# Hybrid encoder trunk on one core: other places for the norm vectors, a later place for the first ReLU tiles, another order of the first weights of the mixers

## The chip, the cores and the metric

The kernel runs on one NeuronCore of a Trainium2 chip. The metric is the device time of one execution in microseconds (us), as the median of several executions. The core has a matrix engine (PE in the profile, TensorE), a vector engine (DVE), a scalar engine (ACT), a general engine (POOL) and an engine that only issues transfers here (SP). They run side by side, each through its own list of instructions in order, and meet only at semaphores: an instruction that waits holds all that stand behind it on its engine.

## What is computed

Two layers of an encoder over 256 tokens of width 1024, in float32. Each layer norms the tokens, feeds three mixers (an mLSTM, a Fourier mixer and a state-space mixer, S5), projects their gated sum, adds it through a second norm, and does the same with a squared-ReLU MLP:

```python
for l in range(DEPTH):                      # DEPTH = 2
    h = rmsnorm(x, g_mix_pre[l])
    z = h @ w_in[l] + b_in[l]               # 1024 -> 5904 columns: q, k, v, o, gates, ...
    ...                                     # y_m, y_f, y_s: mLSTM, Fourier, S5
    mixed = gates[..., 0, :] * y_m + gates[..., 1, :] * y_f + gates[..., 2, :] * y_s
    x = x + rmsnorm(mixed @ w_out[l], g_mix_post[l])
    h = rmsnorm(x, g_ffn_pre[l])
    f = square(relu(h @ w_ffn1[l])) @ w_ffn2[l]     # 1024 -> 4096 -> 1024
    x = x + rmsnorm(f, g_ffn_post[l])
```

## The kernel before

**Products in three parts.** Every float32 factor is split into a high part (`hi`) and a low part (`lo`), and a product is done as hi x hi, hi x lo and lo x hi (`mm3`, lines 273 to 275 of the profile, or the same three in `tokens`, line 289, and `last`, line 311). A weight tile is loaded as `raw` by SP (line 211), copied to `whi` by ACT (line 213), and `wlo` = `raw` - `whi` is done by DVE (line 215). `raw`, `whi` and `wlo` are rings of a few slots: a load waits until DVE has done with the slot it takes, a split until PE has.

**Tokens** are two tiles of 128 rows, t0 and t1. `x_sb` holds x. Where a stage ends, `norms` (lines 397 to 442) does for each tile: a sum of squares of the two halves of the result (ACT, line 405 or 407), the reciprocal root on POOL, the product with the vector of the norm behind the stage (DVE, line 409), the sum into x (line 416), and the product with the vector of the norm ahead of the next stage (line 421, or 377 in a mixer). The normed tile is then turned by eight PE transposes (line 192), whose result is split into `hT_5` (hi) and `hT_6` (lo) by ACT (line 391 or 394) and DVE (line 392 or 395).

**The order there** is written out by hand. `meet` runs over a string, `MEET[0]` at the end of a mixer, `MEET[1]` at the end of an MLP: `0` and `1` are the next step of `norms` for t0 and t1, `P` the products that are left for t1, `h` and `l` the hi and the lo of the next weight tile of the stage that comes (`after`, a `Feed`). In it ACT and DVE follow the written order; elsewhere a scheduler orders the instructions of all engines by its own estimate.

**The start of the MLP.** The first 768 of the 4096 hidden columns are done with the tokens as the standing factor (`tokens`), as a group of 512 (weight tiles in the places `QT0`, `QT1`, `Wt0`, `Wt1`) and a group of 256 (`tabC`/`tabS` and a ring tile), whose splits can be done ahead. For t0 and then t1 the products go to two banks (`mm`), the ReLU to `w2k` (ACT, line 1272), its square (DVE, line 1273), six PE transposes (line 192, out `mm`) turn it, and the result is split into `ringB` (ACT line 1260, DVE line 1261). The rest of the columns (`f1`, chunks of 256) have the weights standing, 48 products of 256 columns each; `f2(kk)` does the second product for 128 hidden columns and both token tiles, 12 products of 512 columns. The scheduler puts `f2` of the first tiles between them.

**The vectors of the norms** are loaded for all partitions (512 KB each) into one pair, a tile of the ring A, by SP at the end of the stage (lines 467 and 470). Ring A has three slots; the S5 loads (lines 637 and 642) take one as well. `Tt`, `oth` and `gx` are places that the mixers use and the MLP does not.

**The first weights of a mixer** (`mixer_units`) are three tiles of the gates and the Fourier columns (`igf`, 272 columns) and four of v (512 columns; 128 x 1024 each), in that order; in layer 1 the first v tile lies in a `whi`/`wlo` slot, the other three in the rings A, A and B.

Of the kernel before, what the change touches and what calls it, by code (L numbers as in the profile page):

```python
# [15 lines left out]
P = 128  # L16
# [40 lines left out]

MEET = ("000Ph11l101", "hl0h0llP0101h11")

# [59 lines left out]
def encoder_kernel(ctx: ExitStack, tc: tile.TileContext, a: dict, out: bass.AP):  # L119
# [152 lines left out]
    def mm3(o, lhi, llo, rhi, rlo, start, stop):  # L272
        mm(o, lhi, rhi, start=start, stop=False)  # L273
        mm(o, lhi, rlo, start=False, stop=False)  # L274
        mm(o, llo, rhi, start=False, stop=stop)  # L275

    def tokens(t, parts, together, step=NK // 2):

        tt = slice(t * P, (t + 1) * P)
        todo = []
        for then, n, units, kn in parts:
            ps = mm_ps()
            o = ps[:, :n]

            def part(a, i, ks, last=False):
                for k in ks:
                    mm(o, a[:, k, tt], units[k // kn][i][:, k % kn, :], start=k == 0 and a is hhi and i == 0,  # L289
                       stop=last and k == NK - 1)  # L290

            for k0 in range(0, NK, step):
                ks = range(k0, min(k0 + step, NK))
                part(hhi, 0, ks)
                if t > 0:
                    part(hhi, 1, ks)
                part(hlo, 0, ks, t > 0)
            if t > 0:
                then(t, ps)
            else:  # L300
                todo.append((then, ps, o, units, kn))
            if not together:
                last(t, todo)
        last(t, todo)
# [77 lines left out]
    def spread(hs, t, scale):  # L382

        for c in range(2):
# [5 lines left out]
            if scale is None:  # L390
                act(o[0], p3, AF.Copy)
                V.tensor_sub(o[1], p3, o[0].bitcast(F32))
            else:
                act(o[0], p3, AF.Copy, scale=scale)
                stt(o[1], p3, scale, o[0].bitcast(F32), ALU.mult, ALU.subtract)

    def norms(t, ps, gpost, gpre, owed=None, lend=None):
# [5 lines left out]
        for c in range(2):  # L403
            if owed is None:
                act(junk(), ps[c], AF.Square, accum_out=ss[:, c:c + 1])
            else:
                act(junk(), ps[c], AF.Square, scale=owed[t][0], accum_out=ss[:, c:c + 1])  # L407
            f = w2k()
            stt(f, ps[c], ROOT_D if owed is None else owed[t][1], gpost[:, half(c)], ALU.mult, ALU.mult)
            fg.append(f)  # L410
        rs = rstd_of(ss)
        yield
# [10 lines left out]
        if lend is not None:  # L423
            yield
            spread(hs, t, None)
            yield
# [35 lines left out]

    def load_gains(gpre, gpost, between=lambda: None):

        gg = ring("A", [P, 2, D])
        if gpost is not None:
            nc.sync.dma_start(gg[:, 1, :], gpost.partition_broadcast(P))
        between()
        if gpre is not None:
            nc.sync.dma_start(gg[:, 0, :], gpre.partition_broadcast(P))  # L470
        return gg
# [562 lines left out]
    def mixer_units(l, iu, vu):  # L1034

        w = a["w_in"][l]
        rings = [None] * 4 if l == 0 else [None, "A", "A", "B"]
        return Feed([(iu, pieces_of(w, k0, min(3, NK - k0), OFF_IG, NIGF)) for k0 in (0, 3, 6)] +
                    [(vu, (*pieces_of(w, k0, 2, OFF_V, M_ML), rings[k0 // 2])) for k0 in range(0, NK, 2)])

    def mixer(l, iu, vu, after, owed):
# [166 lines left out]

        wunits(range(NK))
        gg = load_gains(a["g_ffn_pre"][l], a["g_mix_post"][l], after.load)  # L1210
        for _ in range(5):
            after.lo()
        aps = [[acc_ps(t) for _ in range(2)] for t in range(NT)]

# [38 lines left out]
    def ffn(l, groups, after, owed):  # L1253
# [148 lines left out]
```

## Time and profile before

| what | value |
|---|---|
| median of 3 executions | 836.88 us (836.64 to 836.92) |
| profiled execution | 836.79 us, of which the span of the trace is 835.0 us |
| PE busy in the span | 806.5 us (97%) |
| DVE, ACT, POOL busy | 597.8 (72%), 472.2 (57%), 33.2 us (4%) |
| mean granted clock of PE | 0.995 of full speed |

The table says that PE is the engine whose idle time and clock matter; the others wait most of the time for it or for transfers.

### The profile page before, as it was taken

What the parts mean: (1) busy time and instruction counts of PE and PEld (TensorE: products, weight loads), DVE (VectorE), ACT (ScalarE), POOL (GpSimd) and SP (SyncE); (2) the same over time, 40 slices, a digit from 0 to 9 for tenths busy, and PEclk for the clock granted to TensorE, in tenths of its full rate; (3) what the DMA queues carried; (4) which work ended last, traced back from release to release, by engine and by line L of the source; (5) the groups of instructions that cost most, each with busy time, mean ns of one, the idle gap of its engine ahead of it and who ended that gap; (6) DMA issues with size and microseconds to landing.
All of it is one profiled execution on the core that took longest, in us unless ns stands there. A gap on an engine that the chain in (4) does not pass through costs nothing.

```text
span 835.0 us, 14911 instructions
## 1 busy us (share of the span) xinstructions
PE 806.5 (97%) x5825; PEld 746.1 (89%) x5825; DVE 597.8 (72%) x1071; ACT 472.2 (57%) x784; POOL 33.2 (4%) x63
## 2 busy tenths in 40 slices
PE   7999999998979999999989999999999899999996
PEld 5899999998868999999868999999997699999995
DVE  4999899887783576677568798776987555555563
ACT  4668764676553447567654355666855344444451
POOL 1000200010020000000010010000000100000000
PEclk9999999999999999999999999999999999999999
DMA  8775844554862665756736554555667356666541
GB/s 263 223 225 143 246 121 119 158 163 151 279 176 75 187 191 147 245 166 199 260 111 205 175 178 128 151 177 154 180 200 250 102 171 184 195 184 199 180 176 50
DMA packets 122262, 147.87 MB, mean 177 GB/s; under 512 B 22310, under 2 KB 104398, under 8 KB 121936
## 3 DMA queue, kind: packets, MB, share of 16 engines
q1 hardware_dynamic: 122044, 146.66, 57.5%
q8 instruction: 45, 0.74, 0.4%
q10 hardware_dynamic: 148, 0.27, 0.1%
q14 instruction: 25, 0.20, 0.1%
HBM read 144.33 MB, written 2.57 MB: 176 GB/s over the span
## 4 chain that ended last, share of the span: by engine, by line
issue 43%; PE 24%; DVE 3%; DMA 3%; ACT 2%; POOL 1%; DVEq 0%; POOLq 0%
PE mm L273 5%; PE mm L274 5%; PE mm L275 5%; PE mm L289 3%; DMA raw<-in_w_ffn_dram 2%; DMA raw<-in_w_out_dram 1%; DVE wlo L215 1%; PE acc L793 1%; PE mm L311 1%; PE acc L990 1%; DVE x_sb L416 1%; PE acc L192 1%; POOL rs L358 0%; POOL rs L356 0%; PE acc L829 0%
## 5 line engine op out<-in xcount | busy, mean ns | idle before, releaser
L215 DVE TENSOR_TENSOR wlo<-raw,whi 128x1024 fp32r<-128x1024 f32 (+1 forms) x231 | 280.2, 1217 | 146.9 <-ACT whi L213 145.4
L213 ACT ACTIVATE whi<-raw 128x1024 fp32r<-128x1024 f32 (+1 forms) x231 | 242.1, 1053 | 232.0 <-PE mm L274 139.2
L273 PE MATMUL mm<-hT,whi 128*128 128x256 f32 x1024 | 289.2, 282 | 0.0
L275 PE MATMUL mm<-hT,wlo 128*128 128x256 f32 x1024 | 288.9, 282 | 0.0
L274 PE MATMUL mm<-hT,whi 128*128 128x256 f32 x1024 | 288.7, 282 | 0.0
L273 PEld LDWEIGHTS mm<-hT,whi 128*128 128x128 f32 x1024 | 193.1, 189 | 1.5
L274 PEld LDWEIGHTS mm<-hT,whi 128*128 128x128 f32 x1024 | 192.8, 188 | 1.1
L275 PEld LDWEIGHTS mm<-hT,wlo 128*128 128x128 f32 x1024 | 193.1, 189 | 0.2
L274 PE MATMUL acc<-wlo,ringB 128*128 128x512 f32 x280 | 109.0, 390 | 0.0
L275 PE MATMUL acc<-whi,ringB 128*128 128x512 f32 x280 | 108.3, 390 | 0.0
L273 PE MATMUL acc<-whi,ringB 128*128 128x512 f32 x280 | 107.1, 391 | 0.7 <-ACT ringB L1260 0.7
L275 PEld LDWEIGHTS acc<-whi,ringB 128*128 128x128 f32 x280 | 52.5, 188 | 11.2
L273 PEld LDWEIGHTS acc<-whi,ringB 128*128 128x128 f32 x280 | 52.6, 188 | 11.0 <-ACT ringB L1260 1.0
L274 PEld LDWEIGHTS acc<-wlo,ringB 128*128 128x128 f32 x280 | 52.6, 188 | 9.9
L957 DVE SCALAR_TENSOR_TENSOR t1k<-ringB,pc,t1k 128x254 f32<-128x254 f32 (+1 forms) x64 | 31.0, 484 | 0.9
L289 PE MATMUL mm<-whi,hT 128*128 128x272 f32 (+2 forms) x136 | 29.3, 338 | 1.4 <-ACT whi L213 0.8
L273 PE MATMUL mm<-ringB,whi 128*128 128x256 f32 x96 | 27.4, 286 | 1.7 <-ACT ringB L1027 1.7
L274 PE MATMUL mm<-ringB,whi 128*128 128x256 f32 x96 | 27.3, 284 | 0.0
L275 PE MATMUL mm<-ringB,wlo 128*128 128x256 f32 x96 | 27.2, 284 | 0.0
L356 POOL TENSOR_SCALAR rs<-ss 128x1 f32<-128x1 f32 x16 | 6.6, 415 | 488.6 <-ACT t1k L407 345.7
L289 PEld LDWEIGHTS mm<-whi,hT 128*128 128x128 f32 x136 | 22.2, 202 | 4.2 <-ACT whi L213 1.1
L273 PEld LDWEIGHTS mm<-ringB,whi 128*128 128x128 f32 x96 | 18.3, 191 | 2.0 <-ACT ringB L1027 1.9
(355 smaller groups left out, 1144.0 us busy)
## 6 DMA issues: line engine op xcount, KB each, us to landing
raw<-in_w_ffn_dram SPq DMA_DIRECT2D x128, 512.0 KB
raw<-in_w_in_dram SPq DMA_DIRECT2D x84, 512.0 KB
raw<-in_w_out_dram SPq DMA_DIRECT2D x16, 512.0 KB
raw<-in_w_glu_dram SPq DMA_DIRECT2D x16, 256.0 KB
raw<-in_w_up_mlstm_dram SPq DMA_DIRECT2D x8, 512.0 KB
ringB<-md SPq DMA_DIRECT2D x2, 1024.0 KB
raw<-in_w_up_fourier_dram SPq DMA_DIRECT2D x4, 512.0 KB
raw<-in_w_in_dram SPq DMA_DIRECT2D x4, 408.0 KB
```

The lines of the kernel that those rows point to most:

```text
L192: nc.tensor.transpose(o, i, cst[:k, C_ID:C_ID + k])
L213: act(hi, raw, AF.Copy)
L215: latest[0] = V.tensor_sub(lo, raw, hi.bitcast(F32)).ins
L273: mm(o, lhi, rhi, start=start, stop=False)
L274: mm(o, lhi, rlo, start=False, stop=False)
L275: mm(o, llo, rhi, start=False, stop=stop)
L289: mm(o, a[:, k, tt], units[k // kn][i][:, k % kn, :], start=k == 0 and a is hhi and i == 0, stop=last and k == NK - 1)
L311: mm(o, hhi[:, k, tt], units[k // kn][1][:, k % kn, :], start=False, stop=k == NK - 1)
L416: stt(xv, fg[c], rs, xv, ALU.mult, ALU.add)
L793: mm(bps[:, (g * 2 + r) * JN:(g * 2 + r + 1) * JN], QT[r][:, g0 + g, :], U[:, 4 * b + g, :], start=True, stop=True, skip_group_check=True)
L957: stt(u[:, lo_:hi_], z[:, lo_ + o:hi_ + o], col(l, "cw", j * 8 + i), u[:, lo_:hi_], ALU.mult, ALU.add)
L990: mm(nps[:, d * 256:d * 256 + DH + 1], pt[d, j][:, t * P:(t + 1) * P], v_sb[:, j, h, :], start=i == 0, stop=i == len(js) - 1, skip_group_c ...
```

## The change

No instruction is added or removed; places and orders change.

1. `load_gains` puts each vector into a place of its own: the one behind the mixers into `Tt`, the one ahead of the MLP into `oth`, the one behind the MLP into `oth`, the one ahead of the next mixer into `gx`. SP no longer issues them at the end of the stage, between weight tiles, but as soon as the place is free.
2. `MEET[0]` and `norms`: both sums of squares come first (the product of line 409 stands a step later), and further splits of the MLP's weights stand behind the norms.
3. In the MLP the ReLU tiles of t0 (`done`) and all that follows from them are issued behind all products of t1; those of t1 behind the first `f1` chunk; the sum of squares of x (line 429, `rest`) behind the t0 tiles. `tc.issue_after(i)` only says that what follows stands behind `i` in the schedule.
4. `mixer_units` of layer 1: the first v tile (in ring A) comes second, the next in the `whi`/`wlo` slot; `MEET[1]` splits it ahead of the norms, and the other three between t0's transposes and t1's second norm.

```diff
-MEET = ("000Ph11l101", "hl0h0llP0101h11")
+MEET = ("000P101lh1l1", "hlhl00h0lhlP1001hhh1ll1l1")
...
     def norms(t, ps, gpost, gpre, owed=None, lend=None):
...
+        rs = rstd_of(ss)
+        yield
+        for c in range(2):
             f = w2k()
             stt(f, ps[c], ROOT_D if owed is None else owed[t][1], gpost[:, half(c)], ALU.mult, ALU.mult)
             fg.append(f)
-        rs = rstd_of(ss)
         yield
...
-            spread(hs, t, None)
+            ends[:2] = spread(hs, t, None)
...
-    def load_gains(gpre, gpost, between=lambda: None):
-
-        gg = ring("A", [P, 2, D])
-        if gpost is not None:
-            nc.sync.dma_start(gg[:, 1, :], gpost.partition_broadcast(P))
-        between()
-        if gpre is not None:
-            nc.sync.dma_start(gg[:, 0, :], gpre.partition_broadcast(P))
+    def load_gains(gpost, gpre, tags):
+
+        gg = []
+        for g, tag in zip((gpost, gpre), tags):
+            gg.append(None)
+            if g is not None:
+                gg[-1] = per([P, D], tag)
+                nc.sync.dma_start(gg[-1], g.partition_broadcast(P))
         return gg
...
-        rings = [None] * 4 if l == 0 else [None, "A", "A", "B"]
+        rings = [None] * 4 if l == 0 else ["A", None, "A", "B"]
...
+        if l > 0:
+            specs.insert(1, specs.pop(3))
...
+        gpost, gpre = load_gains(a["g_mix_post"][l], a["g_ffn_pre"][l], ("Tt", "oth"))
         mix = [ring("B", [P, NK, S], F32R) for _ in range(2)]
...
-        for _ in range(5):
+        for _ in range(4):
             after.lo()
+        after.hi()
...
-        parts = [(hidden(f0, n), n, units, kn) for f0, n, kn, units in groups]
+        done = []
+
+        def later(then):
+            return lambda t, ps: done.append((then, t, ps))
+
+        parts = [(later(hidden(f0, n)), n, units, kn) for f0, n, kn, units in groups]
         for t in range(NT):
             tokens(t, parts, True)
+
+        behind = ExitStack()
+        for i in ends:
+            behind.enter_context(tc.issue_after(i))
+        for _ in groups:
+            then, t, ps = done.pop(0)
+            then(t, ps)
+        for chain in owed.pop("rest"):
+            next(chain, None)
...
             f1(c)
+            if c == first:
+                with tc.issue_after(ends[2]):
+                    for then, t, ps in done:
+                        then(t, ps)
+                behind.close()
...
+        gpost, gpre = load_gains(a["g_ffn_post"][l], None if last else a["g_mix_pre"][l + 1], ("oth", "gx"))
```

The changed code has lines of its own: L406, L392, L432 of the change are L405, L391, L429 of before (the sum of squares, hT's hi, the sum of squares of x), L1279 and L1267 are L1272 and L1260 (ReLU, ReLU tile's hi), L290 and L312 are L289 and L311, L274 to L276 are L273 to L275.

**ACT where layer 0 goes from the mixers to the MLP.** Before; `acc_2926` and `acc_2927` are the projection of t0, `acc_2928` and `acc_2929` that of t1, `w2k_3171` is the first ReLU tile:

```order
L405 ACTIVATE t1k_2991,ss_2986<-acc_2927 128x512
L391 ACTIVATE hT_5_84<-acc_3005 128x4x128
L391 ACTIVATE hT_5_84<-acc_3012 128x4x128
L213 ACTIVATE whi_2921<-raw_2920 128x1024
L405 ACTIVATE t1k_3063,ss_3062<-acc_2928 128x512
L405 ACTIVATE t1k_3067,ss_3062<-acc_2929 128x512
L213 ACTIVATE whi_3271<-raw_3270 128x1024
L213 ACTIVATE whi_3301<-raw_3300 128x1024
L213 ACTIVATE whi_3338<-raw_3337 128x1024
L1272 ACTIVATE w2k_3171<-mm_3129 128x512
L391 ACTIVATE hT_5_84<-acc_3082 128x4x128
L391 ACTIVATE hT_5_84<-acc_3089 128x4x128
```

After:

```order
L406 ACTIVATE t1k_2989,ss_2986<-acc_2927 128x512
L406 ACTIVATE t1k_3048,ss_3047<-acc_2928 128x512
L406 ACTIVATE t1k_3050,ss_3047<-acc_2929 128x512
L392 ACTIVATE hT_5_84<-acc_3056 128x4x128
L392 ACTIVATE hT_5_84<-acc_3063 128x4x128
L213 ACTIVATE whi_2922<-raw_2921 128x1024
L392 ACTIVATE hT_5_84<-acc_3083 128x4x128
L392 ACTIVATE hT_5_84<-acc_3090 128x4x128
L1279 ACTIVATE w2k_3200<-mm_3100 128x512
```

Both sums of t1 now stand ahead of t0's hT; three splits that stood ahead of the first ReLU tile are gone from there. They stand here now (`whi_3254`, `whi_3284` of `f1`, `whi_3339`, `whi_3357` of `f2`):

```order
L1279 ACTIVATE w2k_3210<-mm_3117 128x256
L432 ACTIVATE t1k_3236,ss_3233<-x_sb_78 128x512
L213 ACTIVATE whi_3254<-raw_3253 128x1024
L213 ACTIVATE whi_3284<-raw_3283 128x1024
L213 ACTIVATE whi_3339<-raw_3338 128x1024
L213 ACTIVATE whi_3357<-raw_3356 128x1024
L1267 ACTIVATE ringB_3098<-mm_3203 128x4x128
L1267 ACTIVATE ringB_3099<-mm_3213 128x2x128
```

That is ahead of the hi of t0's ReLU tiles (`ringB_3098`, `ringB_3099`), where before nothing stood between the last ReLU and that hi.

**PE at the start of the MLP of layer 0.** Before: from t1's transposes (`acc_3082`, `acc_3089`) to its first products:

```order
L192 MATMUL acc_3082<-cst_79,w2k_3076 128x128 x4
L192 MATMUL acc_3089<-cst_79,w2k_3079 128x128 x4
L311 MATMUL mm_3146<-wlo_2922,hT_5_84 128x256 x4
L192 MATMUL mm_3174<-cst_79,w2k_3171 128x128 x4
L273 MATMUL acc_3265<-whi_3338,ringB_3127 128x512
L274 MATMUL acc_3265<-wlo_3339,ringB_3127 128x512
L273 MATMUL acc_3266<-whi_3338,ringB_3127 128x512
L274 MATMUL acc_3266<-wlo_3339,ringB_3127 128x512
L192 MATMUL mm_3192<-cst_79,w2k_3189 128x128 x2
L289 MATMUL mm_3197<-QT_459_2896,hT_5_84 128x512 x2
```

After: the end of t1's products, t0's ReLU transposes, the first products of `f2`, and the first of `f1` (`mm_3252`):

```order
L290 MATMUL mm_3175<-whi_2922,hT_5_84 128x256 x4
L290 MATMUL mm_3175<-wlo_2923,hT_5_84 128x256 x4
L290 MATMUL mm_3175<-whi_2922,hT_6_85 128x256 x4
L192 MATMUL mm_3203<-cst_79,w2k_3200 128x128 x4
L192 MATMUL mm_3213<-cst_79,w2k_3210 128x128 x2
L274 MATMUL acc_3248<-whi_3339,ringB_3098 128x512
L275 MATMUL acc_3248<-wlo_3340,ringB_3098 128x512
L274 MATMUL acc_3249<-whi_3339,ringB_3098 128x512
L275 MATMUL acc_3249<-wlo_3340,ringB_3098 128x512
L274 MATMUL mm_3252<-hT_5_84,whi_3254 128x256
```

What stood between t1's transposes and its products (ReLU transposes, four products of `f2`) now stands behind the products, and the transposes of t1's ReLU tile are not here but behind the first `f1` chunk and `f2` of t0.

**PE at the start of the mixers of layer 1.** Before; `mm_5148` is the bank of t0's `igf` products, `mm_5174` that of its v products, `acc_5112` and `acc_5119` are t1's transposes:

```order
L289 MATMUL mm_5148<-whi_4918,hT_5_84 128x272 x3
L289 MATMUL mm_5148<-whi_4985,hT_5_84 128x272
L289 MATMUL mm_5148<-whi_4918,hT_6_85 128x272 x3
L289 MATMUL mm_5148<-whi_4985,hT_6_85 128x272
L289 MATMUL mm_5148<-whi_4985,hT_5_84 128x272 x2
L289 MATMUL mm_5148<-whi_5004,hT_5_84 128x272 x2
L289 MATMUL mm_5148<-whi_4985,hT_6_85 128x272 x2
L289 MATMUL mm_5148<-whi_5004,hT_6_85 128x272 x2
L311 MATMUL mm_5148<-wlo_4919,hT_5_84 128x272 x3
L311 MATMUL mm_5148<-wlo_4986,hT_5_84 128x272 x3
L311 MATMUL mm_5148<-wlo_5005,hT_5_84 128x272 x2
L289 MATMUL mm_5174<-whi_5021,hT_5_84 128x512 x2
L192 MATMUL acc_5112<-cst_79,w2k_5108 128x128 x4
L192 MATMUL acc_5119<-cst_79,w2k_5110 128x128 x4
```

After, from t0's first products (`ringA_4987` is the first v tile):

```order
L290 MATMUL mm_5150<-whi_4921,hT_5_84 128x272 x3
L290 MATMUL mm_5150<-whi_4992,hT_5_84 128x272
L290 MATMUL mm_5176<-ringA_4987,hT_5_84 128x512 x2
L290 MATMUL mm_5150<-whi_4921,hT_6_85 128x272 x3
L290 MATMUL mm_5150<-whi_4992,hT_6_85 128x272
```

and from the end of t0's `igf` to t1's transposes (`acc_5127`, `acc_5134`):

```order
L312 MATMUL mm_5150<-wlo_5012,hT_5_84 128x272 x2
L290 MATMUL mm_5176<-whi_5028,hT_5_84 128x512 x2
L290 MATMUL mm_5176<-ringA_4987,hT_6_85 128x512 x2
L290 MATMUL mm_5176<-whi_5028,hT_6_85 128x512 x2
L290 MATMUL mm_5176<-ringA_5101,hT_5_84 128x512 x2
L290 MATMUL mm_5176<-ringB_5105,hT_5_84 128x512 x2
L290 MATMUL mm_5176<-ringA_5101,hT_6_85 128x512 x2
L290 MATMUL mm_5176<-ringB_5105,hT_6_85 128x512 x2
L312 MATMUL mm_5176<-ringA_4987,hT_5_84 128x512 x2
L312 MATMUL mm_5176<-wlo_5029,hT_5_84 128x512 x2
L312 MATMUL mm_5176<-ringA_5101,hT_5_84 128x512 x2
L192 MATMUL acc_5127<-cst_79,w2k_5122 128x128 x4
```

Two products of v stand among the first of `igf`, and v of t0 is all but two products done ahead of t1's transposes, where before two products of v stood.

## Rows read from the trace of the kernel before

**Rows 1.** The page, busy time of an engine, its share of the span, its instructions.

```profile
PE 806.5 (97%) x5825; PEld 746.1 (89%) x5825; DVE 597.8 (72%) x1071; ACT 472.2 (57%) x784; POOL 33.2 (4%) x63
```

**Rows 2.** Waits of PE, whole span: us in total, times, longest.

```profile
PE mm L192 <- DVE w2k L1273: 7.2, 4, 2.7
...
PE acc L192 <- DVE w2k L421: 2.9, 4, 1.1
PE acc L192 <- DVE w2k L377: 2.5, 4, 1.0
```

**Rows 3.** Stretches: us, busy PE, PEld, DVE, ACT, POOL, clock, DMA share, GB/s.

```profile
232.14:243.90 11.76, 9.89 (x61) 8.59 (x61) 9.76 (x14) 6.90 (x12) 0.86 (x2) 1.00 0.39 85
243.90:263.50 19.60, 15.22 (x79) 12.33 (x77) 7.67 (x12) 7.13 (x17) 4.06 (x10) 0.91 0.32 108
...
277.46:283.16 5.70, 5.70 (x49) 5.70 (x48) 2.45 (x2) 2.12 (x2) 0.00 (x0) 1.00 0.58 186
283.16:288.62 5.46, 5.46 (x26) 4.51 (x25) 3.25 (x4) 3.12 (x4) 0.00 (x0) 1.00 0.70 194
640.15:651.03 10.88, 9.89 (x61) 8.57 (x61) 8.91 (x13) 6.89 (x12) 0.86 (x2) 1.00 0.10 40
651.03:669.65 18.62, 15.01 (x80) 12.31 (x78) 7.67 (x12) 7.15 (x17) 4.05 (x10) 0.91 0.35 114
...
429.29:436.20 6.91, 4.86 (x33) 3.95 (x33) 5.15 (x8) 4.31 (x9) 1.95 (x4) 1.00 0.68 208
```

**Rows 4.** Timeline of PE, MLP start of layer 0: start, us, instructions [idle before].

```profile
233.27 0.66 PE L192 MATMUL acc<-cst,w2k 128*128 128x128 f32 x4 [1.14 <-DVE w2k L421]
234.66 0.66 PE L192 MATMUL acc<-cst,w2k 128*128 128x128 f32 x4 [0.73 <-DVE w2k L421]
235.07 1.18 PE L289 MATMUL mm<-QT,hT 128*128 128x512 f32 x4
...
247.29 0.63 PE L192 MATMUL mm<-cst,w2k 128*128 128x128 f32 x4 [2.68 <-DVE w2k L1273]
248.66 0.50 PE L273 MATMUL acc<-whi,ringB 128*128 128x512 f32 x1 [0.74 <-ACT ringB L1260]
```

**Rows 5.** Timeline of ACT, the same place.

```profile
226.85 1.06 ACT L213 ACTIVATE Wt<-raw 128x1024 fp32r<-128x1024 f32 x1 [5.29 <-DMA raw<-in_w_ffn_dram]
228.32 1.06 ACT L213 ACTIVATE tabC<-raw 128x1024 fp32r<-128x1024 f32 x1 [0.40 <-DMA raw<-in_w_ffn_dram]
229.28 0.58 ACT L405 ACTIVATE t1k<-acc 128x512 bf16<-128x512 f32 x1
...
248.01 0.60 ACT L1260 ACTIVATE ringB<-mm 128x512 fp32r<-128x512 f32 x1 [0.48 <-PE mm L192]
```

**Rows 6.** Timeline of DVE, the same place.

```profile
241.92 4.62 DVE L215 TENSOR_TENSOR wlo<-raw,whi 128x1024 fp32r<-128x1024 f32 x4
...
248.64 0.69 DVE L1261 TENSOR_TENSOR ringB<-mm,ringB 128x512 fp32r<-128x512 f32 x1
```

**Rows 7.** Timeline of SP, issues of transfers, 185 to 242 us.

```profile
215.90 0.34 SPq L467 DMA_DIRECT2D ringA<-in_g_mix_post_dram  x1
...
233.18 2.78 SPq L642 DMA_DIRECT2D ringA<-in_s_c_re_dram  x2
```

**Rows 8.** Transfers in all, 217 to 231 us.

```profile
DMA packets 3108, 4.61 MB, mean 329 GB/s; under 512 B 142, under 2 KB 2163, under 8 KB 3106
```

**Rows 9.** Transfers in all, 233.3 to 238.2 us.

```profile
DMA packets 3289, 0.69 MB, mean 141 GB/s; under 512 B 3217, under 2 KB 3217, under 8 KB 3289
...
q1 hardware_dynamic: 3289, 0.69, 69.0%
```

**Rows 10.** Timeline of PE, from the MLP of layer 0 to the mixers.

```profile
430.00 1.32 PE L192 MATMUL acc<-cst,w2k 128*128 128x128 f32 x8 [0.71 <-DVE w2k L377]
...
432.58 1.77 PE L289 MATMUL mm<-whi,hT 128*128 128x272 f32 x12 [0.48 <-DVE hT L395]
...
436.20 0.74 PE L289 MATMUL mm<-whi,hT 128*128 128x512 f32 x2 [0.84 <-ACT whi L213]
```

More of the change, by code (lines that the diff above doesn't have):

```diff
@@ L218, in encoder_kernel @@
     latest = [None]
+    ends = [None] * 3
     def after_weights(l):
@@ L274, in mm3 @@
         mm(o, lhi, rlo, start=False, stop=False)
-        mm(o, llo, rhi, start=False, stop=stop)
+        ends[2] = mm(o, llo, rhi, start=False, stop=stop).ins
     def tokens(t, parts, together, step=NK // 2):
@@ L288, in part @@
                 for k in ks:
-                    mm(o, a[:, k, tt], units[k // kn][i][:, k % kn, :], start=k == 0 and a is hhi and i == 0,
-                       stop=last and k == NK - 1)
+                    ends[2] = mm(o, a[:, k, tt], units[k // kn][i][:, k % kn, :],
+                                 start=k == 0 and a is hhi and i == 0, stop=last and k == NK - 1).ins
             for k0 in range(0, NK, step):
@@ L390, in spread @@
             if scale is None:
-                act(o[0], p3, AF.Copy)
-                V.tensor_sub(o[1], p3, o[0].bitcast(F32))
-            else:
-                act(o[0], p3, AF.Copy, scale=scale)
-                stt(o[1], p3, scale, o[0].bitcast(F32), ALU.mult, ALU.subtract)
+                i = act(o[0], p3, AF.Copy), V.tensor_sub(o[1], p3, o[0].bitcast(F32))
+            else:
+                i = act(o[0], p3, AF.Copy, scale=scale), \
+                    stt(o[1], p3, scale, o[0].bitcast(F32), ALU.mult, ALU.subtract)
+        return [x.ins for x in i]
     def norms(t, ps, gpost, gpre, owed=None, lend=None):
@@ L1036, in mixer_units @@
         w = a["w_in"][l]
-        rings = [None] * 4 if l == 0 else [None, "A", "A", "B"]
-        return Feed([(iu, pieces_of(w, k0, min(3, NK - k0), OFF_IG, NIGF)) for k0 in (0, 3, 6)] +
-                    [(vu, (*pieces_of(w, k0, 2, OFF_V, M_ML), rings[k0 // 2])) for k0 in range(0, NK, 2)])
+        rings = [None] * 4 if l == 0 else ["A", None, "A", "B"]
+        specs = [(iu, pieces_of(w, k0, min(3, NK - k0), OFF_IG, NIGF)) for k0 in (0, 3, 6)] + \
+                [(vu, (*pieces_of(w, k0, 2, OFF_V, M_ML), rings[k0 // 2])) for k0 in range(0, NK, 2)]
+        if l > 0:
+            specs.insert(1, specs.pop(3))
+        return Feed(specs)
     def mixer(l, iu, vu, after, owed):
@@ L1209, in mixer @@
         wunits(range(NK))
-        gg = load_gains(a["g_ffn_pre"][l], a["g_mix_post"][l], after.load)
-        for _ in range(5):
+        for _ in range(4):
             after.lo()
+        after.hi()
         aps = [[acc_ps(t) for _ in range(2)] for t in range(NT)]
@@ L1232, in products @@
                         outproj(k, 1, [c])
-        gpre = [gg[:, 0, half(c)] for c in range(2)]
-        chains = [norms(t, aps[t], gg[:, 1], gpre, lend=owed) for t in range(NT)]
+        chains = [norms(t, aps[t], gpost, [gpre[:, half(c)] for c in range(2)], lend=owed) for t in range(NT)]
         meet(products, *chains, after, MEET[0])
+        owed["rest"] = chains
     GROUPS = ((512, [("QT0",), ("QT1",), ("Wt0",), ("Wt1",)]), (256, [("tabC", "tabS"), None]))
@@ L1323, in ffn @@
             wf2[kk] = wcols(w2, kk, 1, 0, D, in_ring="A")
-        gg = load_gains(None if last else a["g_mix_pre"][l + 1], a["g_ffn_post"][l], after.load)
-        gpre = None if last else [gg[:, 0, half(c)] for c in range(2)]
+        after.load()
+        halves = None if last else [gpre[:, half(c)] for c in range(2)]
         def products(t):
@@ L1336, in products @@
                         f2(kk, [1], [n], lead[-1])
-        chains = [norms(t, aps[t], gg[:, 1], gpre, owed) for t in range(NT)]
+        chains = [norms(t, aps[t], gpost, halves, owed) for t in range(NT)]
         meet(products, *chains, after, MEET[1])
```

## The prediction, made before the changed kernel was run

> **What bounds the kernel now.** I read the page's busy times first: PE works 97% of the span [rows 1], so 835.0 - 806.5 = 28.5 us (with the start and the tail) are all that a change of order can win, beside what a low clock costs. Nothing is taken from PE's work here, and DVE and ACT have much idle time, so their sums say nothing. Next the waits of PE: the largest is for the square of the ReLU tiles, 7.2 us in four waits, then the normed tiles, 2.9 us at the MLP and 2.5 at the mixers [rows 2]. Then the stretches: both starts of an MLP hold these waits. In layer 0 PE idles 11.76 - 9.89 = 1.87 us before its last norm transposes and 19.60 - 15.22 = 4.38 behind them; in layer 1 0.99 and 3.61; the start of layer 1's mixers has 6.91 - 4.86 = 2.05 [rows 3]. [...] At full clock 9% of these stretches would be saved: 0.09 x 19.60 = 1.76 and 0.09 x 18.62 = 1.68 us.
>
> Why PE waits at the ReLU tile is told by the timelines. PE has done t1's norm transposes and wants t0's ReLU tile 2.68 us before it gets it [rows 4]; the square stands on DVE behind four splits that take 4.62 us [rows 6]. Then each hi of the ReLU tile holds PE again, 0.74 us [rows 4], while all 48 products of t1 stand behind on PE's list.
>
> **Part 1, ReLU tiles behind t1's products (both layers).** After the change PE goes from t1's norm transposes straight into t1's 48 products. These take 24 x 5.46/24 for the products of 512 columns and 24 x 5.70/48 for those of 256 [rows 3], 5.46 + 2.85 = 8.3 us, in which ReLU and square of t0 are long done. The 4.38 us (3.61 in layer 1) are gone from there. Three new waits come in their place. (a) The order shows the split of the fourth weight tile ahead of the ReLU tile's hi on ACT; its slot is that of the last tile of t1's products, so it can begin only when these end. It takes 1.05 us, as its kin do [rows 5], then the hi 0.60 [rows 5], 1.65 together, of which six transposes (0.63 for four [rows 4], so some 0.6 before the wait) lie beside: 1.05 us. (b) The first `f1` needs the bank that DVE's lo of that tile frees: behind a split of 1.22 (4.62/4 [rows 6]) and the lo of 0.69 [rows 6], 1.05 + 1.22 + 0.69 = 2.96 us after t1's products, when PE has done transposes, (a) and four products, 0.6 + 1.05 + 0.9 = 2.55: 0.4 us, up to 0.85 if semaphores and the second lo count too. (c) Behind the first `f1` chunk the same happens to t1's tile without a split in front: 0.74 us of idle behind four transposes [rows 4], less the last two transposes (0.3), 0.45 us. In all 1.9 to 2.35; I take 2.1. From below the three are at least 1.0 (the two his less cover), from above 3.6 (each at the size of the waits of [rows 4] and (a)). So 4.38 - 2.1 = 2.3 us in layer 0 and 3.61 - 2.1 = 1.5 in layer 1.
>
> **Part 2, the clock.** In layer 0 the fall lies in the stretch with 2.68 idle, 0.63 transposes and 0.74 idle in a row [rows 4]. The stretch ahead of it had 1.14 and 0.73 us idle around four transposes [rows 4] and kept 1.00 [rows 3]. The new row is 0.6 transposes, 1.05 idle, 0.9 products, 0.4 idle: less idle than the stretch that kept the clock, and broken by products. So I take both falls as gone: 1.76 + 1.68 = 3.4 us. The ends are 0 and 3.4.
>
> [...]
>
> **Part 3, vectors and sums of squares.** Before, two loads of 512 KB for the vectors stand on SP between the third and the fourth tile of the MLP [rows 7], while transfers run at their limit: 4.61 MB in 14 us, 329 GB/s [rows 8]. ACT waits 5.29 us for the fourth tile and 0.40 for `tabC`, and t0's sum of squares stands behind them at 229.28 [rows 5]. Two vectors are 1.05 MB, at 329 GB/s 3.2 us of the queue. They now go where the mixers are still at work. In their place the order shows S5 loads of layer 0: four ahead of the fourth tile and two ahead of `tabC`. The eight of them (four of 32 KB and four of 64 KB, 0.39 MB) are the 3217 short packets of [rows 9]; 69% of 4.9 us is 3.4 us, of which the other 0.30 MB at 329 GB/s take 0.9, so 2.5 for the eight, and I take 2.0 for the six. Net 1.2 us earlier for `tabC`, and so for t0's sums, `x` and transposes. PE's projection ends at 232.14, so the first of the 1.87 us goes and the second stays, with t1's sums now ahead of t0's hT on ACT; first product at 233.9 where it was 235.07 [rows 4]: 1.2 us. In layer 1 no S5 loads stand there, so t0's norm is done before the projection ends; what is left is t1's second sum ahead of the hT: 0.99 becomes about 0.4, 0.6 us. Bounds: 0 where the S5 loads eat all, 1.5 and 0.9 where nothing is left but the hT split. The waits of SP for `Tt`, `oth` and `gx` cost nothing, as these places are last read while mixers run; the splits that moved behind the norms are hidden by t1's 8.3 us of products, and would be late only where they took more (four hi's, 4.2 us).
>
> **Part 4, start of layer 1's mixers.** The 0.71 us for t0's normed tile stays [rows 10]: POOL's root and DVE are as before. The 0.48 for hT's lo is filled by two products of v. The 0.84 for v's first hi [rows 10] goes, since t1's transposes wait behind nearly all products of v; there the lo of the last v tile, behind t1's norm on DVE, I put at 0.4 us. So 2.05 - 0.71 - 0.4, some 1.0 us; bounds 0 (a v tile arrives late, since all loads now come in another order) and 1.4.
>
> **Sum.** Layer 0: 1.2 + 2.3 + 1.76 = 5.2. Layer 1: 0.6 + 1.5 + 1.68 = 3.8. Switch 1.0. In all 10.0 us. The profiled execution took 836.79 (835.0 of span and 1.8 around it), 0.09 under the median: 836.79 - 10.0 = **826.8 us**. With all bounds at their good ends it is about 823.6.
>
> **Rivals.** *A, the clock falls all the same* in one MLP or both: idle then costs as forecast but 1.7 us each come back, 828.5 or 830.2. For it: six transposes and a wait ahead of four products. Against: the stretch that kept 1.00. [...]
> *B, the S5 loads hold the weights of layer 0.* Two of them took SP 2.78 us [rows 7], and short packets move at 141 GB/s [rows 9]. If the fourth tile and `tabC` come 1.5 us later than before rather than 1.2 earlier, ACT's sums come later by as much: 2.7 us, 829.5.
> *C, nothing comes of it*, as the MLP is held by its weight stream and PE waits for tiles later: 836.8. Against: PE has no wait of note in the MLP behind its start, and the largest waits of the trace are not for transfers.
> *D, slower.* SP stands at the first S5 load until its place in ring A is free, and the fourth tile and `tabC` are behind it. The order shows a wait for DVE there; before, the S5 loads came some 17 us behind the vectors [rows 7]. If the place were free only at the end of the projection (232), the fourth tile would be split at about 235.4 and not 226.85: 8.6 later than before, 9.8 later than forecast, with a fall of the clock 826.8 + 9.8 + 1.7 = 838.3. It decides when SP stands more than some 10 us. Against: the place is the one that the vectors took, and they were issued at 215.90 [rows 7].
>
> **Numbers.** Chances: the forecast 0.62 (its own range 825.3 to 828.3), A 0.18, B 0.10, C 0.03, D 0.04, better than the forecast's range 0.03. 823.8 to 830.2 leaves out C, D and a little of A and B. A measurement of this kernel tells 0.2% (1.7 us) from no change; all but C and D are faster by more: faster 0.93, same 0.03, slower 0.04.
>
> **What would show it.** Right: no clock under 1.00 at the MLP starts; no wait for L1273's square of t0; t1's 48 products unbroken; the second `f1` chunk 5 us earlier in layer 0 and 4 in layer 1; a wait of about 1 us ahead of the first `f2` product; t0's sums on ACT ahead of 229. Wrong: a clock of 0.9 there (A); ACT waiting for the fourth tile beyond 226.85 (B, D); waits of PE for `whi` or `wlo` of the splits that moved; a wait for a v tile at the mixers of layer 1.

## The result and the profile after

The changed kernel takes 826.82 us (median of 4 executions, 826.50 to 826.92); the kernel before takes 836.90 (836.64 to 836.97): a ratio of 0.9879 (95% interval 0.9862 to 0.9897). The profiled execution took 826.88 us, its span is 825.1.

The page's first lines and PE's waits in the changed kernel (us in total, times, longest), which answer to [rows 1, 2]:

```profile
span 825.1 us, 14899 instructions
...
PE 804.1 (97%) x5825; PEld 745.4 (90%) x5825; DVE 597.2 (72%) x1071; ACT 471.4 (57%) x784; POOL 36.1 (4%) x63
```

```profile
PE acc L274 <- ACT ringB L1267: 2.9, 4, 1.0
PE acc L192 <- DVE w2k L378: 2.3, 4, 1.1
...
PE acc L192 <- DVE w2k L424: 0.7, 1, 0.7
PE mm L312 <- DVE ringB L215: 0.4, 1, 0.4
PE mm L290 <- ACT hT L392: 0.4, 1, 0.4
PE mm L274 <- DVE ringB L1268: 0.4, 2, 0.2
```

The 7.2 us for the square of the ReLU tiles are gone. In their place stand waits for the hi of these tiles, 2.9 us in four waits, and for the lo that frees a bank, 0.4 in two. The timeline of PE at the MLP start of layer 0 has them one by one: t1's products run unbroken to 252.99, and then

```profile
252.99 0.82 PE L192 MATMUL mm<-cst,w2k 128*128 128x128 f32 x6
254.78 0.50 PE L274 MATMUL acc<-whi,ringB 128*128 128x512 f32 x1 [0.98 <-ACT ringB L1267]
...
256.16 0.39 PE L274 MATMUL mm<-hT,whi 128*128 128x256 f32 x1 [0.18 <-DVE ringB L1268]
...
267.79 0.50 PE L274 MATMUL acc<-whi,ringB 128*128 128x512 f32 x1 [0.47 <-ACT ringB L1267]
273.37 0.28 PE L274 MATMUL mm<-hT,whi 128*128 128x256 f32 x1
```

These are t0's six ReLU transposes, wait (a) of 0.98, wait (b) of 0.18 ahead of the first `f1` chunk, wait (c) of 0.47 for t1's tile, and the second `f1` chunk at 273.37. ACT's timeline names the cause of (a):

```profile
225.43 1.06 ACT L213 ACTIVATE Wt<-raw 128x1024 fp32r<-128x1024 f32 x1 [2.33 <-DMA raw<-in_w_ffn_dram]
228.50 1.06 ACT L213 ACTIVATE tabC<-raw 128x1024 fp32r<-128x1024 f32 x1 [2.01 <-DMA raw<-in_w_ffn_dram]
...
253.19 1.06 ACT L213 ACTIVATE whi<-raw 128x1024 fp32r<-128x1024 f32 x1 [2.26 <-PE mm L290]
254.15 0.85 ACT L1267 ACTIVATE ringB<-mm 128x512 fp32r<-128x512 f32 x2
```

The split of `f2`'s second tile waits for the end of t1's products and stands ahead of the hi. The stretches of the changed kernel (columns as in [rows 3]; the second and third are the MLP start of layer 0 up to the first `f1` product, the next two that of layer 1, the last the start of layer 1's mixers), and under them two of the kernel before:

```profile
188.00:200.00 12.00, 9.46 (x62) 8.74 (x62) 6.62 (x13) 6.17 (x15) 0.00 (x0) 0.86 0.42 146
233.29:244.51 11.22, 10.44 (x65) 9.13 (x65) 8.97 (x13) 3.54 (x7) 1.29 (x2) 1.00 0.32 93
244.51:256.16 11.65, 10.50 (x61) 8.63 (x59) 7.62 (x10) 8.24 (x17) 5.28 (x10) 1.00 0.48 158
634.21:645.00 10.79, 10.40 (x65) 9.08 (x64) 7.66 (x11) 3.45 (x7) 0.86 (x2) 1.00 0.33 101
645.00:656.50 11.50, 10.37 (x59) 8.52 (x58) 7.46 (x10) 8.12 (x17) 5.28 (x10) 1.00 0.53 161
425.20:446.16 20.96, 19.81 (x113) 16.87 (x113) 16.48 (x25) 11.52 (x19) 3.29 (x4) 1.00 0.53 166
```

```profile
188.00:200.00 12.00, 9.46 (x75) 8.75 (x75) 8.11 (x16) 7.69 (x17) 0.00 (x0) 1.00 0.36 113
429.29:452.27 22.98, 20.75 (x113) 16.83 (x114) 19.81 (x36) 12.79 (x20) 1.99 (x4) 1.00 0.65 204
```

The clock is whole at both MLP starts, where [rows 3] had 0.91. But it is 0.86 at 188 to 200 us, where the kernel before had 1.00 around the same two waits (0.75 and 1.74 us in both traces): fewer products got done there (x62 against x75). The forecast did not have that. From the product behind the wait of 1.74 us to the end of the projection PE takes 40.71 us, where it took 39.23, so this fall costs 1.5 us.

Where the time went is read best from start to start, from PE's timelines. "Projection" is the last product of the mixers, "MLP" the first product of `tokens`, "f1" the second `f1` chunk, "S5" the first S5 products of the next mixers.

| stretch | before | changed | forecast gain | gain |
|---|---|---|---|---|
| start to end of projection, layer 0 | 232.14 | 233.29 | 0 | -1.15 |
| projection to MLP, layer 0 | 2.94 | 1.85 | 1.2 | 1.09 |
| MLP to f1, layer 0 | 42.39 | 38.23 | 4.06 | 4.16 |
| f1 to the end of layer 0 | 151.83 | 151.83 | 0 | 0 |
| end of layer 0 to S5 | 22.98 | 20.96 | 1.0 | 2.02 |
| S5 to end of projection, layer 1 | 187.88 | 188.05 | 0 | -0.17 |
| projection to MLP, layer 1 | 2.06 | 1.27 | 0.6 | 0.79 |
| MLP to f1, layer 1 | 41.40 | 38.21 | 3.18 | 3.19 |
| f1 to the last product | 144.96 | 144.96 | 0 | 0 |

The gains sum to 9.9 us, forecast 10.0, but two terms were not as forecast: 1.15 lost ahead of the first MLP, and 1.0 more won at the mixers. And the two stretches from MLP to `f1`, which agree to 0.1 us, hold two parts that do not. Their rows, before and changed (columns as in [rows 3]):

```profile
235.07:277.46 42.39, 38.01 (x215) 32.63 (x214) 23.38 (x30) 20.02 (x35) 4.93 (x12) 0.96 0.38 119
642.20:683.60 41.40, 37.79 (x216) 32.59 (x214) 23.38 (x30) 20.02 (x35) 4.92 (x12) 0.96 0.37 114
```

```profile
235.14:273.37 38.23, 36.61 (x216) 31.63 (x214) 23.13 (x31) 18.56 (x31) 5.62 (x11) 1.00 0.41 126
635.47:673.69 38.22, 36.59 (x213) 31.61 (x213) 23.49 (x31) 18.39 (x31) 5.79 (x11) 1.00 0.41 126
```

PE's idle time fell by 2.76 us in layer 0 (4.38 to 1.62) and by 1.98 in layer 1 (3.61 to 1.63), forecast 2.3 and 1.5; its busy time, in which the clock's price stands, fell by 1.40 and 1.20, forecast 1.76 and 1.68.

### The profile page after: what moved, and what is told of

Its sections match the earlier page's. It is cut to its first block, busy times and chain, and to the rows that moved or that the text cites. A ratio compares the mean times of both kernels' runs of the same rounds, so it can differ in the third digit from the quotient of the medians.

```text
span 825.1 us, 14899 instructions
## 1 busy us (share of the span) xinstructions
PE 804.1 (97%) x5825; PEld 745.4 (90%) x5825; DVE 597.2 (72%) x1071; ACT 471.4 (57%) x784; POOL 36.1 (4%) x63
## 4 chain that ended last, share of the span: by engine, by line
issue 42%; PE 27%; DVE 3%; POOL 2%; ACT 2%; DMA 1%; SPq 0%; DVEq 0%; POOLq 0%
PE mm L274 6%; PE mm L275 6%; PE mm L276 6%; PE mm L290 2%; PE acc L276 1%; PE acc L274 1%; PE acc L275 1%; PE acc L796 1%; DVE wlo L215 1%; PE mm L312 1%; DMA raw<-in_w_ffn_dram 1%; PE acc L993 1%; POOL rs L359 1%; DMA raw<-in_w_out_dram 1%; PE acc L192 1%
## 5 line engine op out<-in xcount | busy, mean ns | idle before, releaser
L274 PE MATMUL mm<-hT,whi 128*128 128x256 f32 x1024 | 289.9, 283 | 0.4 <-DVE ringB L1268 0.4
L276 PE MATMUL mm<-hT,wlo 128*128 128x256 f32 x1024 | 289.5, 283 | 0.0
L275 PE MATMUL mm<-hT,whi 128*128 128x256 f32 x1024 | 289.4, 283 | 0.0
L274 PEld LDWEIGHTS mm<-hT,whi 128*128 128x128 f32 x1024 | 193.7, 189 | 2.7 <-DVE ringB L1268 1.2
L275 PEld LDWEIGHTS mm<-hT,whi 128*128 128x128 f32 x1024 | 193.5, 189 | 1.1
L276 PEld LDWEIGHTS mm<-hT,wlo 128*128 128x128 f32 x1024 | 193.8, 189 | 0.2
L274 PE MATMUL acc<-whi,ringB 128*128 128x512 f32 x280 | 106.7, 392 | 2.9 <-ACT ringB L1267 2.9
L275 PE MATMUL acc<-wlo,ringB 128*128 128x512 f32 x280 | 108.8, 390 | 0.0
L276 PE MATMUL acc<-whi,ringB 128*128 128x512 f32 x280 | 108.1, 390 | 0.0
L274 PEld LDWEIGHTS acc<-whi,ringB 128*128 128x128 f32 x280 | 52.6, 188 | 13.8 <-ACT ringB L1267 3.8
L276 PEld LDWEIGHTS acc<-whi,ringB 128*128 128x128 f32 x280 | 52.4, 188 | 11.1
L275 PEld LDWEIGHTS acc<-wlo,ringB 128*128 128x128 f32 x280 | 52.6, 188 | 10.0
L274 PE MATMUL mm<-ringB,whi 128*128 128x256 f32 x96 | 27.5, 287 | 1.7 <-ACT ringB L1030 1.7
L290 PE MATMUL mm<-whi,hT 128*128 128x272 f32 (+2 forms) x136 | 28.4, 331 | 0.0
L275 PE MATMUL mm<-ringB,whi 128*128 128x256 f32 x96 | 27.4, 286 | 0.0
L276 PE MATMUL mm<-ringB,wlo 128*128 128x256 f32 x96 | 27.4, 285 | 0.0
L290 PEld LDWEIGHTS mm<-whi,hT 128*128 128x128 f32 x136 | 21.9, 198 | 2.7 <-ACT hT L394 0.6
L274 PEld LDWEIGHTS mm<-ringB,whi 128*128 128x128 f32 x96 | 18.5, 192 | 2.0 <-ACT ringB L1030 1.9
```

The lines of the kernel that those rows point to most:

```text
L276: ends[2] = mm(o, llo, rhi, start=False, stop=stop).ins
L290: ends[2] = mm(o, a[:, k, tt], units[k // kn][i][:, k % kn, :], start=k == 0 and a is hhi and i == 0, stop=last and k == NK - 1).ins
```

## The experiments

Times are medians on one chip each; the kernel before, run beside them, took 837.5, 838.2 and 837.3 us on the three chips, with more spread than on the first (835.6 to 840.0, 837.0 to 839.0, 836.2 to 839.2).

**The ReLU part alone** (the kernel before with part 3 of the change, the last step of `norms` taken out of `MEET[0]`).

```diff
-MEET = ("000Ph11l101", ...
+MEET = ("000Ph11l1", ...
+        parts = [(later(hidden(f0, n)), n, units, kn) for f0, n, kn, units in groups]
```

> The kernel before with the ReLU part alone (t0's ReLU tiles behind all products of t1, t1's behind the first f1 chunk); vectors, sums of squares and v tiles as before. Theory 1, the parts add up and the clock's new fall at 193 us is not made by the ReLU part: the gains of the changed kernel's two MLP starts, 4.16 and 3.18 us, come alone, 836.9 - 7.3 = 829.6 us, with PEclk 1.00 at 185 to 200 and at both MLP starts. Theory 2, the ReLU part needs the vectors out of SP's way to pay: at most the clock's 3.4 us, 833.5 us or more.

829.09 us (ratio 0.9899, 0.9878 to 0.9919). MLP to f1 takes 38.28 us in both layers, in the changed kernel 38.23 and 38.21, with a full clock (1.00) there and at 188 to 200 us. Theory 2 falls: the part pays by itself.

**All but the ReLU part.**

```diff
-MEET = ("000P101lh1l1", ...
+MEET = ("000P101lh1l101", ...
-        parts = [(later(hidden(f0, n)), n, units, kn) for f0, n, kn, units in groups]
+        parts = [(hidden(f0, n), n, units, kn) for f0, n, kn, units in groups]
```

> The changed kernel without the ReLU part: vectors in their places, sums of squares and weight splits in the new order, v tiles in the new order. Theory 1, parts add up: first products of the MLPs 1.1 and 0.8 us earlier and the mixers' start 2.0, so 836.9 - 3.9 = 833.0 us, both MLP starts still with a wait of some 2.7 us and a clock of 0.9. If the fall of the clock at 193 us comes with the vector loads (theory 3), 1.6 more, 834.6 us, and the fall is seen there. If the falls at the MLP starts move away with the new position in time, 1.7 less for each.

833.15 us (0.9947, 0.9930 to 0.9963), as the parts add up. The waits for the square are 2.46 and 2.09 us. In its trace the clock stayed whole in layer 0 and fell in layer 1, for twice as long (MLP to f1 39.71 and 43.01 us). There is no fall at 188 to 200 us, though the vector loads are in their new places, so this trace gives nothing for theory 3. The stretch with the fall in layer 1, where the kernel before has a clock of 0.91:

```profile
640.00:660.00 20.00, 16.21 (x73) 12.92 (x72) 10.23 (x14) 5.87 (x15) 3.48 (x10) 0.83 0.48 158
```

**The old order of v.**

```diff
-MEET = (..., "hlhl00h0lhlP1001hhh1ll1l1")
+MEET = (..., "hl00h0llP01101h11")
-        rings = [None] * 4 if l == 0 else ["A", None, "A", "B"]
+        rings = [None] * 4 if l == 0 else [None, "A", "A", "B"]
-        if l > 0:
-            specs.insert(1, specs.pop(3))
```

> The changed kernel with the old order and rings of v's tiles and the old order around them. Theory 1: the start of layer 1's mixers loses the 2.0 us that the stretch gained, 826.8 + 2.0 = 828.8 us, with waits for v's first hi and hT's lo of 0.84 and 0.48 us back. Rival, by idle alone as in the prediction: 826.8 + 1.0 = 827.8 us.

827.46 us (0.9880, 0.9863 to 0.9897). That is less than either forecast, but it was taken on another chip than the changed kernel, so the medians don't decide between 1.0 and 2.0. The stretch does: end of layer 0 to S5 is 22.99 us, as before, with the waits of 0.48 and 0.84 us back, against 20.93 to 20.96 in every trace with the new order.

**Transposes between the groups.** t0's ReLU transposes behind the first group of t1's products, and `f2`'s second split behind that tile.

```diff
+            def put(t, ps):
+                done.append((then, t, ps))
+                if t == 1 and len(done) == 3:
...
+                    for _ in groups:
+                        then_, t_, ps_ = done.pop(0)
+                        then_(t_, ps_)
...
+                    rest.enter_context(tc.issue_after(turned[0]))
...
+                    if 0 < kk < 4:
+                        for i in tile_of[0]:
+                            own.enter_context(tc.issue_after(i))
                     wf2[kk] = wcols(w2, kk, 1, 0, D)
```

> The changed kernel with t0's ReLU transposes between the two groups of t1's products, and the split of f2's second weight tile behind the hi and lo of that tile: nothing should be left for PE to wait for ahead of f2's first products. Theory: waits (a) 0.98 and (b) 0.18 us and the refill of PE behind them go in both layers, 1.3 us each, 826.8 - 2.6 = 824.2 us. Rival, the tile's square or hi is not ready between the groups, so that the wait moves there: 826 us or more.

823.57 us (0.9827, 0.9810 to 0.9844). PE's timeline has the transposes ahead of the second group, and no wait ahead of `f2` or `f1`:

```profile
248.61 0.82 PE L192 MATMUL mm<-cst,w2k 128*128 128x128 f32 x6
249.19 0.72 PE L290 MATMUL mm<-tabC,hT 128*128 128x256 f32 x4
...
251.64 0.64 PE L290 MATMUL mm<-whi,hT 128*128 128x256 f32 x4
252.12 0.63 PE L274 MATMUL acc<-whi,ringB 128*128 128x512 f32 x2
252.59 0.62 PE L275 MATMUL acc<-wlo,ringB 128*128 128x512 f32 x2
253.05 0.28 PE L274 MATMUL mm<-hT,whi 128*128 128x256 f32 x1
```

MLP to f1 is 36.60 and 36.58 us, 1.63 less than in the changed kernel, where the two waits had 1.16: here a wait that went gave more than its idle time, as PE's busy time in the stretch fell too (36.61 to 36.13 us in layer 0). Part of that are the products behind the waits: in the changed kernel 0.50 us behind (a), where the same in a row takes 0.39, and 0.39 behind (b), where it takes 0.28.

**The changed kernel again.** No edit.

> The changed kernel once more, on the chip of the next three. Theory 1, the fall of the clock at 193 us is a matter of the single execution: it is missing in some of these executions (mean clock 0.998 or more beside 0.996), and where it is missing the span is not 1.6 us shorter but some 0.3, since tabC of layer 0 comes no earlier and PE waits for it in its place. Rival: every execution shows the fall, so the change makes it.

826.53 us (0.9864, 0.9850 to 0.9877). The mean clocks are 0.997, 0.999, 0.999 and 0.998. The fall at 193 us is in this trace too (0.997); a clock of 0.86 over 12 us takes 0.002 off the mean of 826 us, so the executions with 0.999 cannot have it, and the first half of theory 1 holds. The second half stays open: here the spans with 0.999 are 823.9 and 825.3 beside 826.4 with the fall, but on the first chip they were 825.0 and 824.7 beside 825.1. What the trace showed beside is the first wait of layer 0, 1.71 us, longer than in the kernel before ([rows 4]: 1.14), since `tabC` came late; timelines of ACT and PE:

```profile
229.77 1.06 ACT L213 ACTIVATE tabC<-raw 128x1024 fp32r<-128x1024 f32 x1 [3.26 <-DMA raw<-in_w_ffn_dram]
```

```profile
234.60 0.66 PE L192 MATMUL acc<-cst,w2k 128*128 128x128 f32 x4 [1.71 <-DVE w2k L424]
235.99 0.66 PE L192 MATMUL acc<-cst,w2k 128*128 128x128 f32 x4 [0.73 <-DVE w2k L424]
```

**The hi first.** Only the second edit of "between".

> The changed kernel with only the split of f2's second weight tile put behind the hi and lo of t0's ReLU tile. Theory: wait (a) falls from 0.98 to about 0.45 us (the hi alone, behind the transposes, as at wait (c)), wait (b) of 0.18 goes; 0.7 us in each layer, 1.4 us less than the changed kernel. Rival, the hi is not what PE waits for: nothing changes.

824.55 us (0.9837, 0.9824 to 0.9850), 2.0 less than the changed kernel on the same chip. Wait (a) is 0.53 and 0.53 us, (b) is gone, MLP to f1 37.33 and 37.37: 0.9 us in each layer.

**Late S5 loads.** The S5 loads that stand at the MLP of layer 0 fetch parameters of layer 1's mixers (hence `l > 0`). Here they go behind later weight tiles of the MLP.

```diff
-            nc.sync.dma_start(dst(raw), src)
+            loaded[0] = nc.sync.dma_start(dst(raw), src).ins
...
+            with tc.issue_after(loaded[0]) if l > 0 else ExitStack():
                 for i, n in enumerate(("s5_b_re", "s5_b_im")):
```

> The changed kernel with the S5 loads of layer 0 behind later weight tiles of the MLP instead of between Wt1 and tabC. Theory of the prediction: these loads take 2.0 us of the queue, so tabC's split comes about 2 us earlier against the end of the projection (6.8 us ahead of it, not 4.8), and layer 0's first waits become those of layer 1 (0.4 us in one piece, not 0.73 + 0.1): 0.4 us less. Rival, the loads cost nothing: tabC stays 4.8 us ahead.

825.83 us (0.9856, 0.9842 to 0.9869). The timelines of ACT and PE:

```profile
226.08 1.06 ACT L213 ACTIVATE tabC<-raw 128x1024 fp32r<-128x1024 f32 x1 [0.36 <-DMA raw<-in_w_ffn_dram]
```

```profile
234.05 1.03 PE L192 MATMUL acc<-cst,w2k 128*128 128x128 f32 x8
235.47 0.74 PE L290 MATMUL mm<-QT,hT 128*128 128x512 f32 x2 [0.39 <-ACT hT L392]
```

`tabC`'s split is now 8.1 us ahead of the end of the projection (234.21), and both norm waits are gone; 0.39 us for `hT`'s hi is left. The median fell by 0.7 us, within the spread of single executions (and this trace has the fall of the clock, 0.72 at 188 to 200 us); that the waits are gone holds in all four traces with late S5 loads (projection to MLP 1.26, 1.26, 1.26, 1.27 us; with the loads between the tiles 1.27 to 3.51 in six traces).

**Both together**, twice.

> Both together: t0's ReLU transposes between the two groups of t1's products, the split of f2's second weight tile behind that tile, and the S5 loads of layer 0 later. Theory, the effects add: 2.6 + 0.4 us less than the changed kernel. Rival: no less than with the transposes alone.

823.03 us (0.9817, 0.9803 to 0.9830), 3.5 us less than the changed kernel on the same chip. The rival is not excluded: the transposes alone had 823.57 on another chip, and the single executions of the two overlap.

> The kernel with the ReLU transposes between the groups and late S5 loads once more, on the chip of the next one: 823 us, with a fall of the clock at 193 us in some executions (mean clock 0.996 beside 0.998).

822.95 us (0.9832, 0.9814 to 0.9850); mean clocks 0.996, 0.996, 0.994, 0.996, with the fall at 193 us in the trace.

**The kernel before, and the ReLU part alone, once more.**

> The kernel before once more, for its trace. Theory 1, the fall of the clock at 189 to 197 us belongs to the single execution: traces of the kernel before can show it too, and the two falls at the MLP starts can be longer or lie elsewhere; mean clock 0.990 to 0.995. Theory 2, the vector loads make it: full clock at 188 to 200 us as in the first trace.

> The kernel before with the ReLU part alone, once more, for its trace. Its vector loads stand where they did before. Theory 1: this kernel had mean clocks of 0.998 and three times 0.996, so its trace can show a fall in the stretch 188 to 200 us. Theory 2: none there, whatever the mean clock.

Single executions: 834.84 us and 828.23. The kernel before shows the fall at 188 to 200 us as well, twice the fall in layer 0 (0.83, in the first trace 0.91) and none in layer 1:

```profile
188.00:200.00 12.00, 9.46 (x62) 8.77 (x62) 6.56 (x14) 6.14 (x14) 0.00 (x0) 0.86 0.31 88
240.00:260.00 20.00, 15.63 (x73) 12.52 (x72) 9.43 (x13) 6.39 (x16) 4.04 (x10) 0.83 0.32 106
640.00:660.00 20.00, 15.95 (x91) 13.35 (x90) 14.41 (x20) 11.51 (x24) 4.92 (x12) 1.00 0.37 121
```

So the fall at 193 us is not made by the change. The trace of the ReLU part shows no fall again, and decides nothing.

**PE kept busy in the wait at 191 us.** The kernel with both edits, and seven products of no use in that wait. Their result is not read; their factors are the normed tokens, not constants.

```diff
+            if l == 0 and h == NH - 1:
+                warm = acc_ps(1)
+                with tc.issue_after(turned[0]):
+                    for _ in range(7):
+                        mm(warm, hhi[:, 0, 0:P], hhi[:, 0:2, :], start=True, stop=True)
```

> The same with seven products of constants of no use (512 columns each, 1.6 us in all, into a bank that nobody reads) put on PE into the wait of 1.74 us at 191 us of layer 0. Theory: the clock falls at 193 us because of that wait, so with PE busy there no execution shows the fall: mean clock 0.998 or more in all, 1.6 us less where the one before has it, the wait itself as long as before. Rival: the fall has another cause, and the mean clocks spread as before.

821.48 us (0.9810, 0.9796 to 0.9824), beside 822.95 on the same chip, which is the 1.5 us of one fall; mean clocks 0.997 to 0.999 in the five executions, where the one beside it had 0.994 to 0.996. One of the five, 0.997, is under the 0.998 that was expected, and a mean does not tell where a clock fell. The stretch and the timeline of PE:

```profile
188.00:200.00 12.00, 11.12 (x82) 10.15 (x83) 8.53 (x16) 6.89 (x13) 0.00 (x0) 1.00 0.55 155
```

```profile
189.09 0.80 PE L192 MATMUL acc<-cst,hm 128*128 128x128 f32 x4 [0.74 <-DVE t1k L1029]
189.64 1.86 PE L1037 MATMUL acc<-hT 128*128 128x512 f32 x7
191.62 0.39 PE L274 MATMUL mm<-ringB,whi 128*128 128x256 f32 x1
```

In the one trace the products fill the wait, and the granted clock is 1.00 at 188 to 200 us. For the other four executions only the mean clock and the time speak, and five of the thirteen traces without these products kept the clock there too (1.00). That PE's idle time in this wait brings the fall is made likely by these five executions, not shown. It is the fastest kernel of the study.

## Why the prediction was right, and where it was not

**ReLU tiles (part 1).** Right in place and kind. The three new waits are where they were put, for the reasons given; "hi first" and "between" take away (a) and (b) by the causes named. They measure 0.98, 0.18 and 0.47, in sum 1.63 us and not 2.1: (b) was mis-sized, 0.18 for 0.4 to 0.85. So the idle time gave 0.5 us more in each layer than forecast.

**Clock at the MLP starts (part 2).** Right: in the eleven traces with the ReLU part no MLP start has a fall, 22 starts in all (1.00 in the rows of the changed kernel above). Of the six starts in the three traces without it four fell. The price was mis-sized: the forecast takes the 9% by which the clock of 0.91 in [rows 3] lies under 1.00 off the time, 1.76 and 1.68 us, and no run shows this relation. What the runs showed is that the second MLP start of the kernel before takes 41.40 us with the fall and 39.98 in the trace without, so a fall costs 1.42 us there, not 1.68. At 188 to 200 us, too, a fall cost 1.5 us where the mean clock of 0.86 makes 0.14 x 12 = 1.7; why it costs less than the mean clock says is not shown. That the MLP stretches came out within 0.1 us is luck: less from the clock, more from the waits. In which execution and layer is not decided by the wait alone: 2.68 us lost the clock in layer 1 of one trace of the kernel before (0.91 over 640 to 660 us) and kept it in the other (1.00). That six transposes ahead of a wait speak for rival A was the author's estimate: with six transposes right ahead of a wait of about 1 us (0.98 in the changed kernel), no trace here shows a fall (twelve places in six traces).

**Vectors (part 3).** The mechanism was right, one price was not. The time from the start of `tabC`'s split to the end of the projection, in all traces, in us:

| | layer 0 | layer 1 |
|---|---|---|
| vectors between the tiles (4 traces) | 3.8 to 5.3, mean 4.7 | 4.7 to 5.4, mean 5.0 |
| S5 loads between the tiles (6 traces) | 3.1 to 5.4, mean 4.6 | (none there) |
| neither (4 traces in layer 0, 10 in layer 1) | 7.0 to 8.6, mean 7.9 | 8.0 to 8.8, mean 8.4 |

The two vectors between the tiles make the split 3.4 us later (layer 1), forecast 3.2. The S5 loads make it 3.3 later, forecast 2.0. So they eat the whole gain in layer 0, and the lower bound of the forecast, 0, is what happens there: projection to MLP is on average 2.1 us with the vectors and 2.0 with the S5 loads. Rival B named the right loads, but its 2.7 us did not come. That the one trace agreed with the forecast (1.09 for 1.2) was chance, as the second trace (3.51) shows. In layer 1, where no S5 loads stand, the pair of traces gives 0.79 for 0.6, and the means of all traces (1.78 with the vectors, 1.26 without) 0.5.

**Start of the mixers (part 4).** Right which waits go and which stay (0.72 stays, 0.40 for the last v tile's lo), wrong in size: 2.02 for 1.0. PE's idle time there fell by 1.08 us, from 2.23 (22.98 - 20.75) to 1.15 (20.96 - 19.81), and its busy time by 0.94 with the same instructions. A product that starts behind a wait is counted as longer than one in a row (0.74 us for two products of 512 columns behind the wait for v's hi [rows 10], 0.63 for two in a row, as in the trace of "between"), and eight transposes that run in one go take 1.03 (the trace with late S5 loads, above) against 1.32 in [rows 10]. These two examples are 0.4 of the 0.94; the rest is not taken apart here. The forecast counted idle time alone.

**The sum.** That it came out within 0.1 us is luck. Mis-sized terms cancelled: +1.0 at the mixers, +0.2 in layer 1's norm, against -1.15 ahead of the first MLP, which is the fall of the clock at 193 us in this one execution (1.5 us), less an earlier start of the product ahead of it (192.57 for 192.91). None of that is in the forecast. Two of its signs missed by this: t0's sums on ACT began at 229.47 and not ahead of 229, and the second `f1` chunk of layer 0 came 4.1 us earlier, not 5.

## What to carry to other kernels

A wait moved behind a long run of products that do not need it is paid by them (here 7.2 us of PE's waits for the square went, and 2.9 for the hi and 0.4 for the lo came); look then at what stands on the other engine's list ahead of what the run ends in (here one split that waited for the run itself: 0.9 us in each layer came back when it stood behind). When a load is taken off a busy queue, see which loads the scheduler lets move up into the hole, and do not price short rows by their bytes alone: here loads of 0.39 MB in short rows made a tile nearly as late as 1.05 MB of vectors did (3.3 and 3.4 us). A clock that falls in some executions and not in others can give or take as much as a small change (here 1.5 us at 193 us, beside 0.7 for the late S5 loads): read it in more than one trace before it is put down to an edit.

## What the runs showed of the hardware

The same kernel with the same waits has a fall of the granted clock in one execution and none in another: the kernel before at 188 to 200 us (1.00 and 0.86), at its second MLP start (0.91 and 1.00 over 640 to 660 us). In slices of 1 us the clock of such a fall reads 0.50 (250 to 252 and 656 to 659 us of the kernel before, 194 to 197 us of the changed one). What decides between them is not shown. A fall of the clock at 193 us cost 1.5 us (from the product behind the wait to the end of the projection 39.19 to 39.23 us in the six traces without a fall, 40.71 to 40.78 in seven with one), and 2.7 us in the one trace where it lasted twice as long (41.93, with a mean clock of 0.72 at 188 to 200 us). Seven products of no use in a wait of 1.74 us went with a whole clock (1.00 at 188 to 200 us) in the one trace taken, and with mean clocks of 0.997 to 0.999 in five executions. The S5 loads, 0.39 MB in packets of under 512 B (six of the eight, 0.26 MB, are issued ahead of `tabC`'s load), put `tabC`'s split 3.3 us later, nearly as much as 1.05 MB of vectors (3.4).
